# A 3x3 convolution in Winograd form: the first input in two pieces, and the first stores behind copies on VectorE

## The chip, the cores and the metric

The kernel runs on one core of one Trainium2 chip. The metric is the device time of one execution in microseconds (us). The kernel before takes 126.59 us, the median of 3 runs (126.56 to 126.64).

A core has five engines with a queue of their own each: TensorE (PE; its weight loads are shown as PEld), VectorE (DVE), ScalarE (ACT), GpSimd (POOL) and SyncE (SP). Transfers are issued from SP, ACT and POOL and are carried out by 16 DMA engines that all of them share.

## The reference

The input `x` is (16, 64, 64, 64) in f32: 16 images, 64 input channels, 64 rows, 64 columns. The weight is (128, 64, 3, 3). The output is (16, 128, 64, 64) in f32.

```
x_pad = np.pad(x, ((0, 0), (0, 0), (1, 1), (1, 1)), mode='constant')
for b, co, ci, kh, kw:
    output[b, co] += weight[co, ci, kh, kw] * x_pad[b, ci, kh:kh+h, kw:kw+w]
```

## The kernel before

**Tiling.** Two images make a pair: their 2 x 64 channels fill the 128 partitions. There are 8 pairs (p = 0 to 7). A pair is worked in 4 blocks (`blk`) of 8 row pairs, which is 16 output rows. Along the rows a small Winograd form is used: the sum of two neighbouring input rows (tile `ss`, f16) is multiplied by the middle weight row (`G1`) and gives U; the odd and even output rows are U plus products of single input rows (tile `xs`, f16) with differences of weight rows (`G21`, `G0` for group A, `G01`, `G2` for group Bt).

**One block** (lines 120 to 182). TensorE computes U (6 matmuls: 3 columns of the weights by 2 images, from `ss`), then A (12 matmuls, from `xs`), then Bt (12 matmuls, from `xs`), each into two PSUM tiles `acc`, one for each image. ScalarE copies U out of PSUM (`ut`, line 164). VectorE adds `ut` to A (line 174) and to Bt (line 177) and writes the f32 result tiles `ot`, one for each image of the pair (64 rows, 2 MB). A block's U needs the row sums of that block; its A and Bt need the f16 rows of the block and one row beyond each end.

**Stores.** When a pair's fourth block is done, SP stores the first image's `ot` (line 181). The second image's store is put into the list `held` and issued on ACT in the next block, behind that block's copies of U (line 171). The last pair is stored in halves.

**Inputs.** Pairs 0 to 3 come as f32 over the SP queue: the weights (line 42), then all of `x0` in one transfer of 2 MB (line 45), then `xf` of pairs 1, 2 and 3 (line 49). Pairs 4 to 7 come over the POOL queue with a cast to f16 on the way straight into `xs` (`load`, line 67): `load(4)` ahead of the pair loop, `load(5)` to `load(7)` in pairs 1 to 3, each behind the row sums that GpSimd makes for the next pair (lines 112 to 116, helper line 76).

**The start.** TensorE transposes the weights (line 93), ScalarE casts them (line 94), then TensorE runs 10 matmuls on zeros (`spin(10)`, line 95). GpSimd makes the two differences of weight rows (lines 96 and 97) and issues `load(4)`. VectorE makes the row sums of all four blocks of pair 0 and ScalarE casts all four pieces of `x0` to f16 (lines 99 to 101), ahead of the pair loop. For pairs 1 to 3 ScalarE casts `xf` in blocks 2 and 3 of the pair before (line 169).

**Order.** `keep` holds an instruction at its written place among the instructions of its engine. Each engine works its queue in that order. `x0`, `xf` and `ot` share one pool of 8 buffers (`opool`, line 36), so that pair 4's results reuse the buffers of pair 0's.

Of the kernel before, what the change touches and what calls it, by code (L numbers as in the profile page):

```python
# [8 lines left out]
F32 = mybir.dt.float32  # L9
# [3 lines left out]
@with_exitstack  # L13
def kernel(
    ctx: ExitStack,
    tc: tile.TileContext,
    x: bass.AP,
    weight: bass.AP,
    out: bass.AP,
):  # L20
    nc = tc.nc
    B, CI, H, W = x.shape
    CO = weight.shape[0]
    assert H == 64 and W == 64 and CI == 64 and CO == 128 and B % 2 == 0
    NP = B // 2
    RB = 8

    keep = tc.keep_in_program_order
    x_rows = x.rearrange("b c h w -> (b c) h w")
    out_rows = out.rearrange("b co h w -> b co h w")  # L30
    w_flat = weight.rearrange("co ci kh kw -> co (ci kh kw)")

    const = ctx.enter_context(tc.tile_pool(name="const", bufs=1))
    psum = ctx.enter_context(tc.tile_pool(name="psum", bufs=8, space=bass.MemoryType.PSUM))
    xpool = ctx.enter_context(tc.tile_pool(name="xpool", bufs=5))
    opool = ctx.enter_context(tc.tile_pool(name="opool", bufs=8))
    spool = ctx.enter_context(tc.tile_pool(name="spool", bufs=3))
    upool = ctx.enter_context(tc.tile_pool(name="upool", bufs=4))


    w_raw = const.tile([CO, CI * 9], F32)
    nc.sync.dma_start(w_raw, w_flat)
    x0 = opool.tile([128, H, W], F32, tag="ot", name="x0")
    cuts = [(0, 18), (18, 34), (34, 50), (50, 64)]
    nc.sync.dma_start(x0, x_rows[0:128, :, :])
    xf = {}
    for p in (1, 2, 3):
        xf[p] = opool.tile([128, H, W], F32, tag="ot", name="xf")
        nc.sync.dma_start(xf[p], x_rows[128 * p : 128 * p + 128, :, :])
    zeros = const.tile([128, 512], F16)  # L50
    keep(nc.vector.memset(zeros, 0.0))  # L51
    warm = psum.tile([128, 512], F32, tag="acc", name="warm")

    def spin(n):
        for _ in range(n):
            keep(nc.tensor.matmul(warm, zeros[:, 0:128], zeros))  # L56

    ident = const.tile([128, 128], F16)
    make_identity(nc, ident)
    w16 = const.tile([CO, CI * 9], F16)  # L60
    keep(nc.gpsimd.tensor_copy(w16, w_raw))  # L61

    xs = {p: xpool.tile([128, H, W], F16, tag="xs", name="xs") for p in range(4)}

    def load(p):
        xs[p] = xpool.tile([128, H, W], F16, tag="xs", name="xs")
        keep(nc.gpsimd.dma_start(xs[p], x_rows[128 * p : 128 * p + 128, :, :]))  # L67

    ss = {}

    def sums(eng, p, src, lo, n):
        if p not in ss:
            ss[p] = spool.tile([128, H // 2, W], F16, tag="ss", name="ss")
        v = src.rearrange("p (j i) c -> p j i c", i=2)
        keep(
            eng.tensor_add(  # L76
                ss[p][:, lo : lo + n, :], v[:, lo : lo + n, 0, :], v[:, lo : lo + n, 1, :]
            )
        )


    Wt = const.tile([128, 5, 3, CO], F16)
    G0, G21, G1, G01, G2 = range(5)

    def wrow(i):
        return Wt[:, i, :, :].rearrange("p t c -> p (t c)")

    for kh, g in ((1, G1), (2, G2), (0, G0)):
        wp = psum.tile([128, 512], F32, tag="acc", name="wp")
        for k in range(3):  # L90
            t = 3 * kh + k
            for q in (0, 64):
                keep(nc.tensor.matmul(wp[q : q + 64, k * CO : k * CO + CO], w16[:, t::9], ident))  # L93
        keep(nc.scalar.copy(wrow(g), wp[:, 0 : 3 * CO]))  # L94
    spin(10)
    keep(nc.gpsimd.tensor_sub(wrow(G21), wrow(G2), wrow(G1)))  # L96
    keep(nc.gpsimd.tensor_sub(wrow(G01), wrow(G0), wrow(G1)))  # L97
    load(4)
    for n, (lo, hi) in enumerate(cuts):
        sums(nc.vector, 0, x0, RB * n, RB)  # L100
        keep(nc.scalar.copy(xs[0][:, lo:hi, :], x0[:, lo:hi, :]))  # L101

    held = []

    def store(eng, p, b2, ot, lo, hi):
        return eng.dma_start(
            out_rows[2 * p + b2, :, lo:hi, :],
            ot.rearrange("p j i c -> p (j i) c")[:, lo:hi, :],
        )

    for p in range(NP):
        if p + 1 < NP:
            for lo in (0, 16):
                sums(nc.gpsimd, p + 1, xf.get(p + 1, xs[p + 1]), lo, 16)
        if p > 0 and p + 4 < NP:
            load(p + 4)
        ots = [
            opool.tile([128, H // 2, 2, W], F32, tag="ot", name="ot") for _ in range(2)
        ]
        for blk in range(4):  # L120
            j0 = blk * RB

            def group(wi_rows):

                tiles = [
                    psum.tile([128, RB, W], F32, tag="acc", name="acc") for _ in range(2)
                ]
                n = 3 * len(wi_rows)
                i = 0
                for wi, off in wi_rows:  # L130
                    for kw in (1, 0, 2):
                        c_lo, c_hi = max(0, 1 - kw), min(W, W + 1 - kw)
                        for b2 in range(2):
                            p0 = 64 * b2
                            lo, hi = j0, j0 + RB
                            if off is None:
                                rhs = ss[p][p0 : p0 + 64, lo:hi, c_lo + kw - 1 : c_hi + kw - 1]
                            else:
                                while 2 * lo + off < 0:
                                    lo += 1  # L140
                                while 2 * (hi - 1) + off > H - 1:
                                    hi -= 1
                                first = 2 * lo + off
                                last = 2 * (hi - 1) + off
                                rhs = xs[p][
                                    p0 : p0 + 64,
                                    first : last + 1 : 2,
                                    c_lo + kw - 1 : c_hi + kw - 1,
                                ]
                            nc.tensor.matmul(  # L150
                                tiles[b2][:, lo - j0 : hi - j0, c_lo:c_hi],
                                Wt[p0 : p0 + 64, wi, kw, :],
                                rhs,
                                start=i == 0,
                                stop=i == n - 1,
                            )
                        i += 1
                return tiles

            U = group([(G1, None)])  # L160
            us = []
            for b2 in range(2):
                ut = upool.tile([128, RB, W], F32, tag="ut", name="ut")
                keep(nc.scalar.copy(ut, U[b2]))  # L164
                us.append(ut)
            if p + 1 in xf:
                q = p + 1
                for lo in {2: (0, 16), 3: (32, 48)}.get(blk, ()):
                    keep(nc.scalar.copy(xs[q][:, lo : lo + 16, :], xf[q][:, lo : lo + 16, :]))  # L169
            while held:  # L170
                keep(store(nc.scalar, *held.pop(0)))
            A = group([(G21, 1), (G0, -1)])
            for b2 in range(2):
                nc.vector.tensor_add(ots[b2][:, j0 : j0 + RB, 0, :], A[b2], us[b2])  # L174
            Bt = group([(G01, 0), (G2, 2)])
            for b2 in range(2):
                nc.vector.tensor_add(ots[b2][:, j0 : j0 + RB, 1, :], Bt[b2], us[b2])  # L177
            parts = {3: (0, 64)} if p < NP - 1 else {1: (0, 32), 3: (32, 64)}
            if blk in parts:
                lo, hi = parts[blk]  # L180
                store(nc.sync, p, 0, ots[0], lo, hi)
                held.append((p, 1, ots[1], lo, hi))
    while held:
        keep(store(nc.scalar, *held.pop(0)))
# [30 lines left out]
```

## Time and profile before

| | |
|---|---|
| median of the runs | 126.59 us |
| span of the profiled execution | 124.8 us |
| PE busy | 108.2 us (87%) |
| DVE busy | 82.8 us (66%) |
| ACT busy | 52.0 us (42%) |
| POOL busy | 36.2 us (29%) |
| moved by DMA | 46.57 MB, mean 373 GB/s |
| read from HBM, written to it | 17.07 MB, 33.55 MB |
| granted TensorE clock, mean | 0.963 |

The profiled execution spans 124.8 us from its first to its last instruction; the runs' time is 1.8 us longer than that, for what lies around the span. The page of the profile gives the busy time of each engine, the span in 40 slices of 3.12 us with tenths of busy time, the DMA queues with their share of the 16 engines, the chain of work that ended last, and groups of instructions. In the queue lines q1 is what SP issues, q10 what ACT issues and q0 what POOL issues. A casting load counts there with the bytes that it writes (1 MB in f16) and not with the 2 MB that it reads. The view by windows gives the same for chosen stretches; the timeline gives instructions in order of time, with the idle time ahead of them and what ended it.

### The profile page before, as it was taken

The page shows a single profiled execution, that of the slowest core. Times are in us where ns is not written, and L with a number is a line of the kernel's source. Part 1 is how long each engine was busy: PE and PEld are TensorE (multiplying, and loading weights), DVE is VectorE, ACT ScalarE, POOL GpSimd, SP SyncE. Part 2 cuts the span into 40 slices and gives each one's busy share as a digit, 9 for nine tenths or more (in the row PEclk, how much of TensorE's full clock was granted, in tenths as well). Part 3 has the DMA queues.
Part 4 walks back from the last instruction along what each step waited for, and adds up shares of the span by engine and source line. Part 5 has one row for each costly group of instructions (what it writes and reads, how often), then busy time and mean ns, then how long its engine had stood idle before and what let it go on. Part 6 is the DMA issues. An engine that isn't in the chain of part 4 may idle for free.

```text
span 124.8 us, 2437 instructions
## 1 busy us (share of the span) xinstructions
PE 108.2 (87%) x988; PEld 49.3 (40%) x988; DVE 82.8 (66%) x133; ACT 52.0 (42%) x84; POOL 36.2 (29%) x27
## 2 busy tenths in 40 slices
PE   0699999999999999999999999999999999990000
PEld 0433444444444444444444444444444444440000
DVE  0016787878878787877777778777877787685000
ACT  4319749833993399333333333333333333330000
POOL 2360086294799202920067000940000000000000
PEclk9999999999999999999999999999999999999555
DMA  6899999999999999999999999999999999999991
GB/s 173 362 436 407 297 323 349 425 315 415 397 349 368 305 376 373 360 334 362 381 347 360 334 344 412 431 431 425 425 441 420 436 415 425 436 412 418 436 402 74
DMA packets 3898, 46.57 MB, mean 373 GB/s; under 512 B 432, under 2 KB 432, under 8 KB 560
## 3 DMA queue, kind: packets, MB, share of 16 engines
q1 hardware_dynamic: 2016, 25.46, 49.5%
q10 hardware_dynamic: 1296, 16.78, 31.6%
q0 software_dynamic: 576, 4.19, 16.1%
q8 instruction: 7, 0.11, 0.3%
q14 instruction: 3, 0.02, 0.0%
HBM read 17.07 MB, written 33.55 MB: 406 GB/s over the span
## 4 chain that ended last, share of the span: by engine, by line
PE 86%; DMA 2%; DVE 1%; issue 1%; POOL 1%; DVEq 0%
PE acc L150 81%; PE warm L56 4%; DMA w_raw<-in_weight_dram 2%; PE wp L93 1%; DVE ot L174 1%; POOL w L61 1%; DVE ot L177 0%; DVEq L210 0%; DVEq L174 0%
## 5 line engine op out<-in xcount | busy, mean ns | idle before, releaser
L150 PE MATMUL acc<-xs,Wt 64*128 64x504 f16 (+3 forms) x768 | 87.0, 373 | 0.0
L150 PEld LDWEIGHTS <-Wt 64*128 64x128 f16 x960 | 46.8, 94 | 56.2 <-issue 0.8
L164 ACT COPY ut<-acc 128x512 f32<-128x512 f32 x64 | 34.3, 588 | 52.9 <-issue 32.1
L174 DVE TENSOR_TENSOR ot<-acc,ut 128x512 f32<-128x512 f32 x64 | 41.2, 686 | 22.6 <-PE acc L150 18.3
L177 DVE TENSOR_TENSOR ot<-acc,ut 128x512 f32<-128x512 f32 x64 | 41.1, 684 | 0.0
L150 PE MATMUL acc<-ss,Wt 64*128 64x504 f16 (+1 forms) x192 | 26.0, 377 | 0.0
L76 POOL TENSOR_TENSOR ss<-xs 128x1024 f16<-128x1024 f16 x8 | 16.8, 2124 | 20.2 <-DMA xs<-in_x_dram 20.2
L76 POOL TENSOR_TENSOR ss<-xf 128x1024 f16<-128x1024 f32 x6 | 14.1, 2361 | 13.6 <-DMA xf<-in_x_dram 13.6
L169 ACT CAST xs<-xf 128x1024 f16<-128x1024 f32 x12 | 12.0, 1058 | 0.0
L76 DVE TENSOR_TENSOR ss<-x 128x512 f16<-128x512 f32 x4 | 2.5, 687 | 7.7 <-DMA x<-in_x_dram 7.7
L93 PE MATMUL wp<-ident,w 128*64 128x128 f16 x18 | 1.3, 328 | 4.3 <-POOL w L61 4.3
L101 ACT CAST xs<-x 128x1024 f16<-128x1024 f32 (+2 forms) x4 | 3.9, 1042 | 2.6 <-DMA x<-in_x_dram 2.6
L67 POOL DMA_DIRECT2D xs<-in_x_dram x4 | 2.4, 600 | 7.8 <-ACT xs L169 7.8
L56 PE MATMUL warm<-zeros 128*128 128x512 f16 x10 | 4.4, 631 | 0.0
L93 PEld LDWEIGHTS <-w 128*64 128x64 f16 x18 | 1.1, 210 | 4.3 <-POOL w L61 4.3
L94 ACT CAST Wt<-wp 128x384 f16<-128x384 f32 x3 | 1.2, 487 | 2.9 <-PE wp L93 2.9
L56 PEld LDWEIGHTS <-zeros 128*128 128x128 f16 x10 | 1.3, 143 | 2.3 <-issue 2.2
L94 ACT ACT_TABLE_LOAD x1 | 1.3, 1283 | 0.7 <-PEq L199 0.7
L96 POOL TENSOR_TENSOR Wt<-Wt 128x384 f16<-128x384 f16 x1 | 0.9, 907 | 1.7 <-ACT Wt L94 1.7
L61 POOL CAST w<-w_raw 128x576 f16<-128x576 f32 x1 | 0.7, 663 | 2.3 <-DMA w_raw<-in_weight_dram 2.3
L97 POOL TENSOR_TENSOR Wt<-Wt 128x384 f16<-128x384 f16 x1 | 0.9, 910 | 0.0
L51 DVE MEMSET zeros<- 128x256 uint32 x1 | 0.3, 272 | 0.9 <-PEq L199 0.9
(6 smaller groups left out, 0.9 us busy)
## 6 DMA issues: line engine op xcount, KB each, us to landing
out_dram<-ot SPq DMA_DIRECT2D x7, 2048.0 KB, 22.0
out_dram<-ot ACTq DMA_DIRECT2D x7, 2048.0 KB, 18.9
xf<-in_x_dram SPq DMA_DIRECT2D x3, 2048.0 KB, 22.1
xs<-in_x_dram POOLq DMA_DIRECT2D x4, 1024.0 KB, 23.4
x<-in_x_dram SPq DMA_DIRECT2D x1, 2048.0 KB, 7.6
out_dram<-ot SPq DMA_DIRECT2D x2, 1024.0 KB, 10.6
out_dram<-ot ACTq DMA_DIRECT2D x2, 1024.0 KB, 11.0
w_raw<-in_weight_dram SPq DMA_DIRECT2D x1, 288.0 KB, 2.8
```

What stands on the lines that cost most here:

```text
L56: keep(nc.tensor.matmul(warm, zeros[:, 0:128], zeros))
L61: keep(nc.gpsimd.tensor_copy(w16, w_raw))
L67: keep(nc.gpsimd.dma_start(xs[p], x_rows[128 * p : 128 * p + 128, :, :]))
L76: eng.tensor_add(ss[p][:, lo : lo + n, :], v[:, lo : lo + n, 0, :], v[:, lo : lo + n, 1, :])
L93: keep(nc.tensor.matmul(wp[q : q + 64, k * CO : k * CO + CO], w16[:, t::9], ident))
L94: keep(nc.scalar.copy(wrow(g), wp[:, 0 : 3 * CO]))
L101: keep(nc.scalar.copy(xs[0][:, lo:hi, :], x0[:, lo:hi, :]))
L150: nc.tensor.matmul(tiles[b2][:, lo - j0 : hi - j0, c_lo:c_hi], Wt[p0 : p0 + 64, wi, kw, :], rhs, start=i == 0, stop=i == n - 1,)
L164: keep(nc.scalar.copy(ut, U[b2]))
L169: keep(nc.scalar.copy(xs[q][:, lo : lo + 16, :], xf[q][:, lo : lo + 16, :]))
L174: nc.vector.tensor_add(ots[b2][:, j0 : j0 + RB, 0, :], A[b2], us[b2])
L177: nc.vector.tensor_add(ots[b2][:, j0 : j0 + RB, 1, :], Bt[b2], us[b2])
```

## The change

- `x0` comes in two transfers, rows 0 to 17 and rows 18 to 63, on the same SP queue.
- Of the matmuls on zeros 6 stand ahead of the weight transposes and 2 behind them, in place of 10 behind.
- A GpSimd copy of one column out of row 63 of `x0` (`hold`) stands ahead of `load(4)`, which thereby waits for the second piece of `x0`.
- Of the four row sums and four casts of pair 0, only the first of each stands ahead of the pair loop. Each of the others is made one block ahead of its use, inside pair 0: the cast on ACT behind the copies of U, the sum on VectorE between the adds of A and the adds of Bt.
- The adds of A and Bt get `keep`.
- Pair 0's two stores are not issued at its end. In pair 1, block 1, behind the first add of A, VectorE copies one element column of each of pair 0's two result tiles onto itself; then SP stores the first tile and, behind the second add, ACT the second.

```diff
-    nc.sync.dma_start(x0, x_rows[0:128, :, :])
+    for lo, hi in ((0, 18), (18, H)):
+        nc.sync.dma_start(x0[:, lo:hi, :], x_rows[0:128, lo:hi, :])
...
+    spin(6)
     for kh, g in ((1, G1), (2, G2), (0, G0)):
...
-    spin(10)
+    spin(2)
     keep(nc.gpsimd.tensor_sub(wrow(G21), wrow(G2), wrow(G1)))
     keep(nc.gpsimd.tensor_sub(wrow(G01), wrow(G0), wrow(G1)))
+    hold = const.tile([128, 1], F32)
+    keep(nc.gpsimd.tensor_copy(hold, x0[:, H - 1, 0:1]))
     load(4)
-    for n, (lo, hi) in enumerate(cuts):
-        sums(nc.vector, 0, x0, RB * n, RB)
+
+    def first_cast(n):
+        lo, hi = cuts[n]
         keep(nc.scalar.copy(xs[0][:, lo:hi, :], x0[:, lo:hi, :]))
 
+    sums(nc.vector, 0, x0, 0, RB)
+    first_cast(0)
+
     held = []
+    gate = []
...
+            if p == 0 and blk < 3:
+                first_cast(blk + 1)
...
             for b2 in range(2):
-                nc.vector.tensor_add(ots[b2][:, j0 : j0 + RB, 0, :], A[b2], us[b2])
+                keep(nc.vector.tensor_add(ots[b2][:, j0 : j0 + RB, 0, :], A[b2], us[b2]))
+                if gate and blk == 1 and b2 == 0:
+                    for ot in gate:
+                        end = ot[:, H // 2 - 1, 1, W - 1 : W]
+                        keep(nc.vector.tensor_copy(end, end))
+                    store(nc.sync, 0, 0, gate[0], 0, H)
+                    held.append((0, 1, gate[1], 0, H))
+                    gate = []
+            while p == 1 and held:
+                keep(store(nc.scalar, *held.pop(0)))
+            if p == 0 and blk < 3:
+                sums(nc.vector, 0, x0, j0 + RB, RB)
             Bt = group([(G01, 0), (G2, 2)])
             for b2 in range(2):
-                nc.vector.tensor_add(ots[b2][:, j0 : j0 + RB, 1, :], Bt[b2], us[b2])
+                keep(nc.vector.tensor_add(ots[b2][:, j0 : j0 + RB, 1, :], Bt[b2], us[b2]))
...
-            if blk in parts:
+            if blk == 3 and p == 0:
+                gate = ots
+            elif blk in parts:
```

## The prediction

> **What bounds the kernel now.** I read the page first. Its chain of waits gives TensorE 86% of the span, but the slices say otherwise:
>
> ```profile
> PE   0699999999999999999999999999999999990000
> DMA  6899999999999999999999999999999999999991
> q1 hardware_dynamic: 2016, 25.46, 49.5%
> q10 hardware_dynamic: 1296, 16.78, 31.6%
> q0 software_dynamic: 576, 4.19, 16.1%
> PE 86%; DMA 2%; DVE 1%; issue 1%; POOL 1%; DVEq 0%
> ```
>
> TensorE stops four slices before the end; the DMA engines are full from the third slice to the last but one, and the three queues' shares sum to 97.2%. Windows show how full:
>
> ```profile
> 1.00:2.00 1.00, 0.00 (x0) 0.00 (x0) 0.13 (x1) 1.00 (x1) 0.29 (x1) 1.00 0.23 44
> 24.00:26.00 2.00, 2.00 (x22) 0.98 (x20) 1.40 (x3) 0.70 (x2) 1.70 (x1) 1.00 1.13 442
> 26.00:28.00 2.00, 2.00 (x22) 0.88 (x18) 1.39 (x3) 1.07 (x2) 2.00 (x2) 1.00 0.94 246
> 30.00:32.00 2.00, 2.00 (x22) 0.93 (x20) 1.27 (x4) 1.97 (x4) 0.16 (x1) 1.00 1.02 434
> 115.00:120.00 5.00, 0.00 (x0) 0.00 (x0) 0.00 (x0) 0.00 (x0) 0.00 (x0) 0.57 1.01 428
> ```
>
> The last two columns are the DMA share and GB/s. VectorE is done at 113.9 us; from there to 124.8 us only transfers run, at 428 GB/s, so the two last stores (2.1 MB, 4.9 us at that rate) stand behind older ones. **The transfers are the bound:** the change leaves their bytes alone, so the end moves only with time in which the 16 engines stand idle or run slowly. TensorE has slack: the bytes left at 113.9 us take some 9 us, of which 4.9 us are the last stores' own, so it could end about 4 us later.
>
> One stretch is slow: 26 to 28 us moves 246 GB/s at a full share. Against 430 that loses 0.9 us, and 28 to 29 us (328 GB/s) another 0.2: 1.1 us in all. The queue view explains when stores begin:
>
> ```profile
> DMA packets 22, 0.20 MB, mean 393 GB/s; under 512 B 10, under 2 KB 10, under 8 KB 10
> ## 3 DMA queue, kind: packets, MB, share of 16 engines
> q1 hardware_dynamic: 21, 0.18, 85.8%
> q10 hardware_dynamic: 1, 0.02, 7.6%
> ```
>
> This is 28.5 to 29 us: the first ACT store packet, though ACT issued it at 24.30. From 26 to 28 us only q1 moves, with loads. So pair 0's stores, issued early, wait in their queues until the loads are through and follow without a gap. By bytes: the windows sum to 11.27 MB by 32 us; loads are 9.73 MB of it, 0.03 is instructions. The 1.5 MB of stores take 3.5 us at 430 GB/s: **stores effectively start at 28.5 us.** From there to the end both kernels move the same bytes without a pause. So I forecast one time: when the stores' first bytes move after the change.
>
> **The change, part by part.** The rows I use:
>
> ```profile
> 1.17 0.42 SPq L45 DMA_DIRECT2D x<-in_x_dram  x1
> 8.80 2.50 DVE L76 TENSOR_TENSOR ss<-x 128x512 f16<-128x512 f32 x4 [7.67 <-DMA x<-in_x_dram]
> 9.92 0.82 PE L150 MATMUL acc<-ss,Wt 64*128 64x512 f16 x6
> 16.33 0.81 PE L150 MATMUL acc<-ss,Wt 64*128 64x512 f16 x6
> 18.55 1.29 DVE L174 TENSOR_TENSOR ot<-acc,ut 128x512 f32<-128x512 f32 x2 [0.47 <-PE acc L150]
> 23.70 0.35 SPq L106 DMA_DIRECT2D out_dram<-ot  x1
> 28.11 1.29 DVE L174 TENSOR_TENSOR ot<-acc,ut 128x512 f32<-128x512 f32 x2 [0.73 <-PE acc L150]
> 31.84 4.68 POOL L76 TENSOR_TENSOR ss<-xf 128x1024 f16<-128x1024 f32 x2 [2.35 <-DMA xf<-in_x_dram]
> ```
>
> *The first piece of x0.* The weights land at about 3.5 us. 18 rows are 0.59 MB, 1.4 us at 430 GB/s: landed near 4.9. The second piece lands where the whole did, 8.8; the extra issue costs SP 0.42 us, hidden while the DMA is backed up. Sum 0 (0.69 us) ends at 5.6. ACT's three weight casts end at 6.2, its cast of 18 rows (1.15) at 7.35. The transposes end at 5.6, two spins (0.43 each) at 6.4: first U at 6.4, not 9.92. The six spins ahead run from about 1.2 to 3.8, while PE waits for the weights until 4.30. A begins at 7.35, after the cast (G21 is ready at 6.82).
>
> *Pair 0 then runs by VectorE.* Each later U needs its sum, and VectorE makes that behind both adds of A. From a U to the first A add is 2.22 us (16.33 to 18.55), both adds 1.29, the sum 0.69 less 0.05 overlap, the hand-over about 0.1 (an estimate from the 0.05 to 0.1 us between such rows): 4.2 us a block, where Us stand 3.24 apart now (13.09, 16.33, 19.58). A add 0: A begins at 7.35, 12 matmuls and the tail of the last take about 1.5: 8.8; adds to 10.05, sum 1 to 10.7, U of block 1 at 10.8 (13.09 before). Blocks 2 and 3: 15.0 and 19.2. Pair 1: 22.4 and, block 1, 25.6, against 22.74 and about 25.9. The early start is given back almost entirely; TensorE ends 0.3 us earlier, in its slack.
>
> *The gate.* Pair 1's first A add in block 1 ends at 25.6 + 2.22 + 0.68 = 28.5; then two copies of one column. The trace has none on VectorE: below, nothing; above, the 0.27 us of its memset; I take 0.1 each, like GpSimd's 128x1 memsets, which are the nearest in size. They delay the second add inside the 0.73 us that VectorE idles there. SP issues at 28.6. From issue to the first bytes: the weights were issued at 0.74 on empty queues, and the window 1 to 2 us holds a share of 0.23, so data moves from 1.77: 1.0 us. **First store bytes at 29.6, 1.1 us later than the 28.5 of now.** The loads, if the slow stretch goes with the early stores, end at 27.4, and the engines stand empty for 2.2 us; if it stays, at 28.5 and for 1.1. The end is the same.
>
> *Other waits.* Behind the gated store SP has only pair 1's store (36.5). ACT waits until 28.7 with nothing behind but the U copies of block 2, ready after 29.4. POOL's copy waits until 8.8, so `load(4)` goes out 1.3 us later (7.63 before); pair 4 needs it past 60 us, and meanwhile xf fills the engines. That copy's own time, 0.1 to 0.66 us by GpSimd's nearest rows, lies in POOL's wait for xf. `load(5)` stands behind sums that wait for xf, issued near 28.9 as now, too late to fill the hole. Casts: block 2 holds ACT for 1.07 + 0.93 + 2 x 1.0 = 4.0 us, within 4.2. If xf of pair 1 came late here, TensorE's slack pays, but the gate moves with it. Pair 4 reuses pair 0's buffers near 60 us; their stores land about 1 us after 45.7, no wait.
>
> *Clock.* TensorE spins 0.43 us apart up to 9.37 and runs 512 columns in 0.21 from 9.92: full speed 5.1 to 5.6 us after its first work at 4.30. From 1.2 us on that gives 6.3 to 6.8, so U and some of A may run at half: 0 to 0.6 us later at the gate; I take 0 and keep 0.6 for the range. The Trainium skill's page TensorE: Matmul & The Clock Gate, Part 1, states that a free-running window of about 3.4 us has to be busy first: by it, as an estimate, full speed comes one to two windows after the first work, at 4.6 to 8.0 us, and the sum is 1.1 or, at 8.0, 1.7; the 5.1 to 5.6 us of this trace lie between one and two windows.
>
> Span: 124.8 + 1.1 = 125.9. The profiled span lies 1.8 us below the runs' median; with that, **127.7 us**, 0.9% slower.
>
> **Rivals.** *Faster: the slow stretch goes and no hole opens.* If sums and adds on VectorE don't hold pair 0 and Us stand 3.24 apart from 10.0, the gate's add ends at 10.0 + 2 x 3.24 + 3.2 + 3.2 + 2.9 = 25.8; stores queue up by 26.8, ahead of the loads' end at 27.4. Then the 1.1 us come back: 125.5. It decides at the gate: SP's issue before 26.4. For it: the slow stretch begins some 1.5 us after the first two stores' issue and never recurs. Against: 2.22, 1.29 and 0.69 are firm rows in one chain. Chance 0.18.
>
> *Same: late engines set the end.* One transfer is done only when the slowest of 16 engines is; pair 3's xf releases POOL at 31.84, 2.8 us after q1 turned to stores elsewhere. An engine with loads left until past 29.6 has no hole, and if it also ends last, the end stays: 126.6. Against: its loads share it with stores from 28.5, so its real lag is about half. The Trainium skill's DMA: Bandwidth & Descriptors, Latency and other measured facts, says engines 7 and 15 are usually slower; the 31.84 fits one slow engine, but not which. Chance 0.12.
>
> *Much slower: the pieces don't act as pieces.* If sum 0 waits for all of x0, U starts at 9.9 again, A's adds end at 13.5, U of block 1 is at 14.3, all 3.5 us later: 127.7 + 3.5 = 131.2. For it: a wait may cover a whole tile; against: A started at 10.58, before ACT's last cast into the same xs. Chance 0.12.
>
> **Numbers.** Forecast 0.58, its own range 127.1 (late engines absorb half of 1.1) to 128.8 (1.1, and 0.6 for the clock, 0.2 for a dearer copy, 0.3 for hand-overs of 0.2 three times). The range takes in the faster case and leaves out 131.2: 125.5 to 128.8. By over 0.2% (0.25 us, about what a measurement here can tell): faster 0.18, same 0.12, slower 0.70.
>
> **What would show it.** Right: Us of pair 0 near 6.4, 10.8, 15.0, 19.2; DVE, not PE, as releaser before them; SP's first store near 28.6; a window near 28 to 29.5 us with a low DMA share and TensorE busy; from 30 us full shares to the end. Wrong: full shares through 27 to 30 us, store issue before 26.4, or an end that no longer follows the DMA.

## The result, and the profile after

The kernel after takes 131.2 us (median of 4 runs, 130.51 to 131.37) against 126.58 us before: a ratio of 1.0358, interval 1.0341 to 1.0376. It is 4.6 us slower, where 1.1 us were forecast; the time lies above the range. The profiled execution spans 129.6 us against 124.8. Medians and ranges here are of all executions, ratios of the fast ones alone, because some executions of the same kernel, of the kernel before too, are over 1.5% longer.

Lines from the page of the kernel after: slices and chain.

```profile
PE   6897649999999999999999999999999999980000
DVE  0109694687878777877778778777877787772000
PEclk9999995999999999999999999999999999999755
DMA  4999999964999999999999999999999999999990
PE 81%; DVE 5%; DMA 2%; issue 2%; POOL 1%; DVEq 0%
```

Two things are new. The DMA row, full throughout before, drops to 6 and 4 in the ninth and tenth slice (26 to 32 us, at 3.24 us a slice). And TensorE is weak in the fourth to sixth (7, 6, 4; 10 to 19 us), with a slice of low clock behind it; in the chain VectorE has 5% in place of 1. The timeline shows where this comes from:

```profile
11.06 0.68 DVE L77 TENSOR_TENSOR ss<-x 128x512 f16<-128x512 f32 x1
...
15.07 5.10 POOL L77 TENSOR_TENSOR ss<-xf 128x1024 f16<-128x1024 f32 x2 [4.67 <-DMA xf<-in_x_dram]
15.21 2.75 DVE L77 TENSOR_TENSOR ss<-x 128x512 f16<-128x512 f32 x1
...
18.01 0.82 PE L159 MATMUL acc<-ss,Wt 64*128 64x512 f16 x6 [2.80 <-DVE ss L77]
...
23.19 0.82 PE L159 MATMUL acc<-ss,Wt 64*128 64x512 f16 x6
...
32.51 0.35 SPq L115 DMA_DIRECT2D out_dram<-ot  x1
```

The same row sum on VectorE takes 0.68 us at 11.06 and 2.75 us at 15.21, just behind GpSimd's first row sum. TensorE waits 2.80 us for it. The next block then takes 5.2 us (18.01 to 23.19) in place of the 4.2 forecast, and SP issues the first store at 32.51, not 28.6. The windows give the clock and the transfers; the last three columns are granted clock, DMA share and GB/s:

```profile
16.00:18.00 2.00, 0.00 (x0) 0.00 (x0) 2.00 (x2) 0.00 (x0) 2.00 (x2) 1.00 1.01 311
...
20.00:22.00 2.00, 2.00 (x12) 0.75 (x10) 0.76 (x2) 2.00 (x3) 0.17 (x1) 0.50 1.08 332
...
26.00:28.00 2.00, 2.00 (x22) 0.96 (x20) 1.90 (x4) 1.80 (x4) 2.00 (x2) 1.00 0.96 410
28.00:30.00 2.00, 2.00 (x24) 0.92 (x20) 1.51 (x3) 0.32 (x1) 2.00 (x2) 1.00 0.08 33
30.00:32.00 2.00, 2.00 (x22) 0.93 (x20) 1.27 (x3) 1.07 (x2) 1.98 (x2) 1.00 0.64 61
...
34.00:36.00 2.00, 2.00 (x22) 0.88 (x18) 1.36 (x3) 2.00 (x4) 1.55 (x2) 1.00 0.97 176
```

From 16 to 18 us TensorE does nothing; from 20 to 22 us it runs at half clock (12 matmuls in place of 22). From 28 to 31 us the DMA engines are almost empty: the loads are through, the stores not yet issued. Then comes a surprise: the stores are issued at 32.5, but from 32.5 to 36.5 us the queues hold this:

```profile
DMA packets 90, 0.75 MB, mean 186 GB/s; under 512 B 0, under 2 KB 0, under 8 KB 0
## 3 DMA queue, kind: packets, MB, share of 16 engines
q0 software_dynamic: 89, 0.73, 102.9%
q8 instruction: 1, 0.02, 1.5%
```

Only `load(5)` moves (POOL issued it at 29.76). The first store packet starts at 36.9 us, 4.4 us behind its issue. (A casting load counts with the bytes that it writes: 16 engines with packets of 8 KB at 0.62 us make 211 GB/s, so 186 is near what this load can show.) Weighing each packet by the usual duration of its kind (0.61 us for 16 KB, 0.62 us for 8 KB of a casting load), the engines lose some 4.5 us between 28 and 38 us; before, they lost about 1 us in the slow stretch and next to nothing from there to the tail. A further 0.6 us against the kernel before is lost from 2 to 6 us, where the first piece of `x0` moves in smaller packets (1.27 MB in these 4 us against 1.53). Together that is some 4.1 us of the 4.8 us by which the span grew; the rest I can't place.

### The profile page after: what moved, and what is told of

Its sections match the earlier page's. It is cut to its first block, busy times and chain, and to the rows that moved or that the text cites. A ratio compares the mean times of both kernels' runs of the same rounds, so it can differ in the third digit from the quotient of the medians.

```text
span 129.6 us, 2437 instructions
## 1 busy us (share of the span) xinstructions
PE 110.7 (85%) x986; PEld 49.5 (38%) x986; DVE 85.3 (66%) x135; ACT 52.0 (40%) x84; POOL 37.3 (29%) x28
## 3 DMA queue, kind: packets, MB, share of 16 engines
q10 hardware_dynamic: 1296, 16.78, 30.5%
## 4 chain that ended last, share of the span: by engine, by line
PE 81%; DVE 5%; DMA 2%; issue 2%; POOL 1%; DVEq 0%
PE acc L159 79%; DVE ss L77 3%; DMA w_raw<-in_weight_dram 2%; DVE ot L185 2%; PE wp L95 1%; PE warm L57 1%; POOL w L62 1%; DVE ot L199 0%; DVEq L234 0%; DVEq L185 0%
## 5 line engine op out<-in xcount | busy, mean ns | idle before, releaser
L159 PE MATMUL acc<-xs,Wt 64*128 64x504 f16 (+3 forms) x768 | 89.0, 380 | 0.0
L159 PEld LDWEIGHTS <-Wt 64*128 64x128 f16 x960 | 47.5, 96 | 62.3 <-issue 4.3
L173 ACT COPY ut<-acc 128x512 f32<-128x512 f32 x64 | 34.4, 589 | 58.7 <-issue 37.7
L159 PE MATMUL acc<-ss,Wt 64*128 64x504 f16 (+1 forms) x192 | 26.7, 385 | 3.6 <-DVE ss L77 3.6
L77 DVE TENSOR_TENSOR ss<-x 128x512 f16<-128x512 f32 x4 | 4.8, 1201 | 4.8 <-DMA x<-in_x_dram 4.8
L57 PE MATMUL warm<-zeros 128*128 128x512 f16 x8 | 3.8, 628 | 1.2 <-DVE zeros L52 1.2
```

The costliest lines, as they stand in the source:

```text
L77: eng.tensor_add(ss[p][:, lo : lo + n, :], v[:, lo : lo + n, 0, :], v[:, lo : lo + n, 1, :])
L159: nc.tensor.matmul(tiles[b2][:, lo - j0 : hi - j0, c_lo:c_hi], Wt[p0 : p0 + 64, wi, kw, :], rhs, start=i == 0, stop=i == n - 1,)
```

## The experiments

For reference, the start of the first stores in all the kernels, in us. "Bytes" is the start of the first store packet in the trace's DMA records; in the kernels that issue ahead of 28 us (before, e1, e4, e6, e8, e9) it is that of ACT's first large store, since SP's stores can't be told from its loads there. Issue, bytes and span are of the one profiled execution, the time is the median of all. The profiled execution took less than its median in e2 (128.43), e5 (130.43) and e13 (130.11), and more in e3 (129.1) and e9 (128.17).

| kernel | SP issue | load(5) issue | bytes | span | time |
|---|---|---|---|---|---|
| before | 23.70 | 28.93 | 28.6 | 124.8 | 126.58 |
| e4, a small store early | 23.44 | 29.09 | 28.3 | 124.6 | 126.64 |
| e6, extra instructions | 23.35 | 29.29 | 28.1 | 124.9 | 126.63 |
| e1, all but the gate | 24.53 | 29.71 | 28.7 | 124.6 | 126.73 |
| e9, x0 in pieces alone | 24.56 | 30.25 | 28.7 | 126.4 | 126.67 |
| e8, gate a block earlier | 26.06 | 28.93 | 28.1 | 125.9 | 127.56 |
| e2, gate alone | 28.61 | 29.14 | 29.5 | 126.7 | 129.04 |
| e3, sums early | 28.95 | 29.38 | 29.8 | 127.3 | 127.77 |
| e10, turns taken | 29.12 | 29.59 | 30.0 | 127.4 | 129.22 |
| e5, spins in the wait | 29.62 | 29.69 | 30.5 | 128.4 | 131.68 |
| e11, later start | 30.10 | 29.57 | 34.3 | 129.0 | 130.75 |
| e12, the same and spins | 30.20 | 29.71 | 34.4 | 129.1 | 131.01 |
| e13, e11 with load(5) later | 30.10 | 34.68 | about 31 | 128.3 | 131.06 |
| after | 32.51 | 29.76 | 36.9 | 129.6 | 131.2 |
| e7, after with load(5) later | 32.74 | 34.70 | 33.6 | 131.0 | 129.66 to 134.0 |

### e1: all of the change but the gate

```diff
-            while p == 1 and held:
-                keep(store(nc.scalar, *held.pop(0)))
...
-            if blk == 3 and p == 0:
-                gate = ots
-            elif blk in parts:
+            if blk in parts:
```

> The kernel after, without the wait of pair 0's stores: they are issued at the end of pair 0 again (SP near 27.3 us, since pair 1 starts at 26.4 there). Theory L: the first stores of the program move their first bytes some 4.6 us after issue whatever stands in the queues (4.6 us in the kernel after), so near 31.9 us, and the DMA engines stand empty from 28.4 to there: 127.8 us (127.2 to 128.8). Rival Q: the 4.6 us came of the casting load that stood in the queues, and stores alone start 1.0 us after issue: near 28.4 us, no hole, 126.9 us.

126.73 us, ratio 1.0024 (0.9981 to 1.0066): the same as before. SP issued at 24.53 us and not at 27.3, because pair 0 ended earlier here: the sum of block 2 began at 14.22 us, ahead of GpSimd's (15.12), and took 0.68; the sum of block 3 fell under GpSimd's second and took 1.94:

```profile
15.12 4.67 POOL L77 TENSOR_TENSOR ss<-xf 128x1024 f16<-128x1024 f32 x2 [4.68 <-DMA xf<-in_x_dram]
...
18.39 1.94 DVE L77 TENSOR_TENSOR ss<-x 128x512 f16<-128x512 f32 x1
```

(The 4.6 us of the expectation are 4.4 by the packet records.) There was no hole, as rival Q has it, but the stores stood behind loads, so that this run doesn't decide between L and Q. It shows that the new order of pair 0, one slow sum included, costs nothing measurable by itself; it acts through the gate.

### e2: the gate alone

The kernel before, with the diff's lines of `gate` and nothing else.

> The kernel before with the wait of pair 0's stores alone. TensorE's course stays (pair 1, block 1 near 25.9 us), SP issues near 28.9 us. Theory L: first bytes near 33.5 us, the loads end near 27.4, the casting load that POOL issues at 28.9 fills part of the hole: 130.3 us (129 to 131). Rival Q, stores start 1.0 us after issue: near 29.9 us, 128.0 us.

129.04 us, ratio 1.0207 (1.0143 to 1.0271). First store bytes come at 29.5, 0.9 us behind SP's issue: theory L falls, Q stands, and the forecast of 1.0 us from issue to first bytes was right. But 1.0 us of later stores cost 1.8 to 3.4 us of time. The windows, of the fastest of the four executions (128.43 us), show where:

```profile
28.00:30.00 2.00, 2.00 (x22) 1.08 (x20) 2.00 (x6) 0.24 (x1) 1.98 (x3) 1.00 0.38 147
30.00:32.00 2.00, 2.00 (x22) 1.06 (x20) 1.36 (x3) 2.00 (x4) 2.00 (x1) 1.00 0.97 401
...
34.00:36.00 2.00, 2.00 (x22) 1.09 (x20) 1.68 (x3) 1.96 (x3) 1.98 (x3) 1.00 0.79 205
```

The slow stretch has left 26 to 28 us, but another stands at 34 to 36 (205 GB/s), just ahead of the first packets of `load(5)` at 35.5. From 26 to 36 us the engines lose some 2.4 us against 1.0 before, and a few tenths more up to 50, which is about what this execution is longer. That `load(5)` causes the slow stretch is not shown.

### e3: the row sums out of GpSimd's way

```diff
-            if p == 0 and blk < 3:
-                sums(nc.vector, 0, x0, j0 + RB, RB)
+            if p == 0 and blk == 0:
+                for n in (1, 2, 3):
+                    sums(nc.vector, 0, x0, n * RB, RB)
```

> The kernel after with the three later row sums of pair 0 made one behind the other in block 0, ahead of GpSimd's first row sum. Theory: the sum of 2.75 us was slow because GpSimd read SBUF at the same time. Then all four take 0.69 us, Us of pair 0 stand near 6.7, 11.8, 15.1 and 18.3 us, TensorE's clock stays full, SP issues near 27.7 us. With theory L first bytes near 32.3 us and 128.3 us; with rival Q first bytes near 28.7 us and 127.0 us. If the slow sum has another cause, one of the three is slow again.

127.77 us, ratio 1.0114 (1.005 to 1.0178): 3.4 us below the kernel after. The three sums together take 1.89 us; the Us stand at 7.4, 13.2, 16.4 and 19.6. In the execution that was traced, the longest of the four (129.1 us), the first sum is the slow one (1.40 us at 5.93, beside GpSimd's weight differences), and the first U and A run at half clock (7.5 to 10.9 us); SP issues 1.3 us later than expected. The first sum meets the weight differences in every trace of the kernel after and its variants: where it begins first (after, e1, e5, e7) it takes 0.69 us and the difference beside it 1.27 to 1.40 in place of 0.91, and where the difference begins first (e3, e10, e11, e12, e13) the sum takes 1.21 to 1.41.

### e10: the same sums, taken in turns

```diff
+    turn = const.tile([128, 1], F16)
...
-        if p + 1 < NP:
+        if 0 < p < NP - 1:
...
+            if p == 0 and blk == 2:
+                keep(nc.gpsimd.tensor_copy(turn, ss[0][:, H // 2 - 1, 0:1]))
+                for lo in (0, 16):
+                    sums(nc.gpsimd, 1, xf[1], lo, 16)
```

> The kernel after, with GpSimd's first row sums put behind VectorE's last row sum of pair 0 (a copy of one column of that sum on GpSimd makes them wait); nothing else is moved. If the two engines' turns at SBUF are what made the gate late, all of VectorE's sums take 0.7 us, pair 1 starts near 22.5 to 23.5 us, SP's first store is issued near 28.6 to 29.6 us on empty engines, its first bytes move 0.9 us later, and the time is 127.7 to 129 us, with a full clock from 12 us on. GpSimd's sums for pair 1 then end near 22.3 us for the first half, just in time. If TensorE's idle time has another cause: 131.2 us.

129.22 us, ratio 1.0153 (1.0076 to 1.0229), 2.0 us below the kernel after. No instruction of VectorE was moved, and its sums of blocks 2 and 3 are quick:

```profile
14.89 0.68 DVE L77 TENSOR_TENSOR ss<-x 128x512 f16<-128x512 f32 x1
...
19.06 0.68 DVE L77 TENSOR_TENSOR ss<-x 128x512 f16<-128x512 f32 x1
...
19.95 4.69 POOL L77 TENSOR_TENSOR ss<-xf 128x1024 f16<-128x1024 f32 x2
```

The sum of block 2 proves little, since at 14.89 us it began ahead of the time (15.0 to 15.2) at which GpSimd's first sum begins in the other kernels. The sum of block 3 does: in e11 below, where GpSimd's two sums were left in place (15.22 to 20.17), the same sum begins at nearly the same time and is slow:

```profile
19.12 1.60 DVE L77 TENSOR_TENSOR ss<-x 128x512 f16<-128x512 f32 x1
```

So it is GpSimd's sum beside it that makes VectorE's slow.

### e6: the two engines' turns by themselves

```diff
+            if p in (1, 6) and blk in (0, 3):
+                extra = const.tile([128, RB, W], F16, name=f"extra{p}{blk}")
+                if blk == 0:
+                    keep(nc.vector.tensor_add(extra, us[0], us[1]))
+                else:
+                    keep(nc.vector.tensor_scalar_mul(extra, us[0], 2.0))
```

> The kernel before with four extra instructions on VectorE, 512 elements each, whose results are not used: in pair 1 and in pair 6, an add of two SBUF tiles in block 0 and a product of one SBUF tile with 2 in block 3. GpSimd makes row sums beside those of pair 1 and nothing beside those of pair 6. Theory (two SBUF inputs on VectorE and a GpSimd instruction that reads SBUF take turns): the add takes 0.7 us in pair 6 and 1.0 to 2.9 us in pair 1, or GpSimd's sum is longer by as much; the one-input product is a smaller question: the same time in both pairs if one input never waits. Rival (the slow sum came from x0 or from its place in the queue): the add takes 0.7 us in both.

```profile
24.22 5.12 POOL L76 TENSOR_TENSOR ss<-xf 128x1024 f16<-128x1024 f32 x2 [4.08 <-DMA xf<-in_x_dram]
...
25.74 1.38 DVE L178 TENSOR_TENSOR extra<-ut 128x512 f16<-128x512 f32 x1
...
35.45 1.60 DVE L180 TENSOR_SCALAR extra<-ut 128x512 f16<-128x512 f32 x1
...
89.76 0.68 DVE L178 TENSOR_TENSOR extra<-ut 128x512 f16<-128x512 f32 x1
...
99.48 0.42 DVE L180 TENSOR_SCALAR extra<-ut 128x512 f16<-128x512 f32 x1
```

The add takes 1.38 us beside GpSimd's sums and 0.68 without; GpSimd's two sums take 5.12 us in place of 4.69. The one-input product waits too: 1.60 against 0.42. The adds that read PSUM (1.29 for two) keep their time beside GpSimd throughout. The rival, that `x0` or the place mattered, falls. The times say how the two share: in the kernel after, e1, e11 and here, VectorE's sum or add ends 0.55 us after the end of the GpSimd sum that had begun before it (here 27.12 us after 26.57), whenever it began itself.

### e5, e11, e12: the clock

e5 puts 8 matmuls on zeros into TensorE's wait (the first hunk); e11 starts later by 4 zeros matmuls in place of 2 (the second); e12 has both.

```diff
+            if p == 0 and blk == 2:
+                again = psum.tile([128, 512], F32, tag="acc", name="again")
+                for _ in range(8):
+                    keep(nc.tensor.matmul(again, zeros[:, 0:128], zeros))
...
-    spin(2)
+    spin(4)
```

> The kernel after with 8 matmuls on zeros ahead of U of block 2 in pair 0, where TensorE stood idle for 2.8 us and then ran at half clock from 18.9 to 22.5 us. If the clock fell because of that idle time, it stays full here: U of block 3 comes near 22.3 us instead of 23.2, SP's first store near 31.6 instead of 32.5, and the time falls by 0.5 to 0.9 us against the kernel after, to 130.3 to 130.7 us. If the clock does not matter to the end: 131.2 us. The slow sum stays in either case.

> The kernel after with 4 matmuls on zeros in place of 2 behind the weight transposes: the first U comes some 0.4 to 0.9 us later, so that the sum for block 2 always starts behind GpSimd's row sum of 15.1 us. If that sum's start against GpSimd's decides, it takes 2 us or more as in the kernel after, TensorE waits about 2.8 us and its clock falls to half again: 131.2 to 132 us, SP's first store near 32.5 to 33 us.

> The same with 8 matmuls on zeros ahead of U of block 2 in pair 0, inside the wait for the slow sum. The slow sum stays; if the clock fell because of the idle time, it stays full now, pair 0 ends 0.9 to 1.9 us earlier than in the kernel with the later start alone, and the time lies 0.5 to 1.5 us below that kernel's. If the clock has no part in the end: the same time.

131.68 us for e5 (ratio 1.0392, 1.0323 to 1.0462), 130.75 for e11 (1.0322, 1.0275 to 1.0369), 131.01 for e12 (1.0346, 1.0303 to 1.0389). The expectations failed in their premise: in the profiled executions of e5 and e12 no sum of blocks 2 and 3 was slow, and in e11 only that of block 3 was (1.60 us at 19.12). With 4 zeros matmuls the first U came 0.7 us later (7.45 us, held up by a first sum of 1.25 us), but it ran at full clock, so that the first A add came at 9.58 and not behind 9.85. So these runs don't isolate the clock's share. They show something else: in e11 the clock stays full, SP issues at 30.10, 2.4 us earlier than in the kernel after, and the time is almost the same. What e11, e12 and the kernel after share is that `load(5)` was issued ahead of the stores.

### e7 and e13: load(5) out of the stores' way

```diff
-        if p > 0 and p + 4 < NP:
-            load(p + 4)
+        if p == 2:
+            load(5)
+        if p > 1 and p + 4 < NP:
+            load(p + 4)
```

> The kernel after with load(5) issued together with load(6), so that no casting load stands in the queues when pair 0's stores are issued near 32.5 us. Theory Q (a transfer starts 1.0 us after issue on empty engines, and some 4 us after issue behind another queue's work): first store bytes near 33.5 us instead of 36.9. The engines then stand empty from 28.5 to 33.5 us, 5 us against the 4.5 us lost in the kernel after: 131 to 132 us. If the 4.4 us belong to the stores themselves: first bytes near 37 us, and 134 to 135 us.

> The kernel with 4 matmuls on zeros in place of 2 (SP issued its first store at 30.1 us there, 0.5 us behind load(5), and stores moved from 34.3 us on: 130.75 us), with load(5) issued together with load(6) as well. If the order of load(5) and the first stores costs time of its own, stores move from 31.0 us on, the engines lose 3.0 to 3.5 us between 28 and 36 us in place of 4.3, and the time is 129.5 to 130 us. If only the time of the gate matters, since load(5) has to be moved at some time anyway: 130.75 us or more.

In e7, traced in a run of 132.81 us, SP issues at 32.74 and the first bytes move at 33.6, 0.9 us later, and so do they in e13 (30.10 to 31.0): the 4.4 us belong to the queues, not to the stores. The runs of e7 spread from 129.66 to 134.0 us, so its time decides nothing. In e13, with the gate at e11's time, the engines lose some 2.5 us between 28 and 36 us in place of 4.3, as the first theory had it; but between 36 and 50 us they lose over 1 us more than in e11, when `load(5)` starts behind the stores. The time, 131.06 us (ratio 1.0363, 1.0323 to 1.0404), can't be told from e11's. So no cost of the order by itself shows: in both, the engines stand empty from 28 us until something is issued, and lose time again when the other starts.

### e4, e8 and e9: the slow stretch

e4 is the kernel before with one small store into the output issued on ACT at the start; e8 is e2 with `blk == 0` for `blk == 1`; e9 is the kernel before with `x0` in two pieces and nothing else.

> The kernel before with one store of 64 bytes a partition into the output, issued on ACT at the start (those 16 columns are written again by the last store). Theory L in the form that the first store into the output is slow and slows what runs beside it: the slow stretch at 26 to 28 us goes, pair 0's stores follow the loads at 27.5 us, 125.5 us. If the delay belongs to each large store or to the queues' first large store: the slow stretch stays, 126.6 us.

> The kernel before with the copies and pair 0's stores one block earlier than in the change, in block 0 of pair 1: SP issues near 25.5 us, while the loads still run until 27.4. In the run without the gate stores issued at 24.5 us had no slow stretch. If the slow stretch depends on issue while more than about 4 us of loads stand queued, it goes, no hole opens, and the time is 125.7 us. If the stores start some 4 us after issue as they do behind loads, near 29.5 us, a hole of up to 2 us opens and takes the place of the slow stretch: 126.5 to 127.5 us.

> The kernel before with x0 loaded in the two pieces of 18 and 46 rows and nothing else. In the kernel after the engines moved 355 GB/s from 4 to 6 us against 401 before. If the pieces themselves cost that, some 0.5 us are lost there: 127.1 us; the slow stretch at 26 to 28 us stays. If the loss came of something else at the start: 126.6 us.

e4: 126.64 us, ratio 1.0008 (0.9983 to 1.0034), and the slow stretch stays (287 GB/s from 26 to 28 us): it does not hang on the first store into the output. e8: 127.56 us with a wide spread (126.25 to 128.5; ratio 1.0034, 0.9995 to 1.0073), so not faster. No hole opens at 28 us and the slow stretch is gone there, but 0.4 us are lost from 32 to 36 and 0.5 from 36 to 50. e9: 126.67 us, ratio 0.9994 (0.9964 to 1.0023). In its trace the pieces cost some 0.6 us from 2 to 6 us, and the slow stretch at 26 to 28 us is gone (401 GB/s). That the one pays for the other would fit the equal times, but is not shown: the execution traced here was 1.5 us longer than the median. e1, which has the pieces too and was traced in a run of 126.43 us, shows both:

```profile
2.00:4.00 2.00, 1.93 (x5) 0.45 (x3) 0.00 (x0) 0.01 (x1) 0.33 (x1) 1.00 0.99 298
4.00:6.00 2.00, 1.61 (x19) 1.26 (x20) 0.20 (x1) 0.96 (x3) 0.35 (x2) 1.00 1.03 345
...
26.00:28.00 2.00, 2.00 (x22) 0.88 (x18) 2.00 (x4) 0.37 (x1) 2.00 (x2) 1.00 0.97 401
```

The kernel before moves 363, 401 and 246 GB/s in these three windows. The pieces don't do away with slow stretches as such: e3 and e10 have one at 34 to 36 us (262 and 266 GB/s), as e2 has. What the slow stretch is stays open; no kernel tried was faster than the one before.

## Why the prediction was wrong

**What held.** The direction, and the way to it: a late gate and a hole in the transfers. The transfers are the bound: TensorE's last work and VectorE's (117.5 us) again lie 12 us ahead of the end. The early start is given back: in e10, with quick sums, the Us are 4.2 us apart as forecast (11.47, 15.63, 19.80), and pair 1 starts at 22.97 where 22.4 was forecast and 22.74 stood before. The hole, and its place from 28 us on, came as forecast. A store issued on empty engines moves its first bytes 0.9 us later (e2, e3, e7, e10), against 1.0.

**The step that failed: "the sum 0.69 less 0.05 overlap".** The duration was read from the row at 8.80 us, beside which GpSimd makes nothing, and moved to a place beside GpSimd's row sums of pair 1, which I had in view only as a consumer of xf. There it took 2.75 us. The Trainium skill's page SBUF — State Buffer, section SBUF: two separate sides, says that a VectorE instruction with two SBUF inputs and a GpSimd instruction that reads SBUF take an exclusive lock on a shared pair of ports, and that the one that comes second is blocked for the whole instruction of the other. This trace agrees: GpSimd's first sum runs from 15.07 to 17.40 us; VectorE's, begun at 15.21, ends at 17.96, 0.55 us later. I didn't look for it. With the sums out of each other's way the time is 2.0 us (e10) to 3.4 us (e3) lower, of the 3.5 us by which the forecast was too low. The step fails at the forecast's own times too: there the sum of block 3 begins near 18.4 us, where e1's took 1.94.

**The clock, taken at 0 with 0.6 in reserve.** TensorE's matmuls came 0.43 us apart until 8.8 us, through U and the first third of A, and 0.21 apart from there on; the first A add came at 9.85, not 8.8. In e1 they were 0.21 us apart from U's start at 6.55 us on, and the add came at 8.87. That one us moved the sum of block 2 from ahead of GpSimd's sum (14.2 in e1) to behind it (15.21): a small term decided which sum was caught. The second fall of the clock, from 19.0 to 22.4 us, followed the 2.8 us wait and wasn't in the prediction; it makes the block 5.2 us long where e10's blocks take 4.2. No run isolates its effect on the time.

**The gate.** Together these put SP's issue at 32.51 in place of 28.6. The Us of pair 0 show the parts: block 1 stands at 11.79 where 10.8 was forecast (1.0 us, the start), block 2 at 18.01 for 15.0 (2.0 us more, the slow sum), block 3 at 23.19 for 19.2 (1.0 us more, the half clock); the 4 us then stay up to the gate.

**"From there to the end both kernels move the same bytes without a pause."** In e2 the first bytes moved 1.0 us later than before, and the time rose by 2.6 (1.8 to 3.4); a slow stretch stood again at 34 to 36 us, when `load(5)` started behind the stores. So even with the gate at the forecast's time the 1.1 us forecast were too few, by some 1.5 us. In the kernel after it worked the other way: from 28.5 to 36.9 us is 8.4 us, but only some 4.5 us were lost, since `load(5)`, which I had called too late for the hole, moved in it.

**The rivals.** *Much slower* gave 131.2 us, the time that was measured, by coincidence: its mechanism did not occur, for the first sum began at 5.94 us, right behind the first piece. *Faster* failed where it was said to be decided, at the gate (26.4). *Same* had no part: the hole shows in the mean of all engines.

## What to carry to other kernels

A duration moves with its neighbours: before an instruction is put somewhere else, look at what the engine that shares its ports does at that time, not only at whether its own inputs are ready. Where transfers are the bound, a wait ahead of a store is safe only while something else still stands in the queues; a gate on a compute chain moves with that chain, here by 4 us, and later stores cost more than their delay (e2). A wait on the transfer's own progress was not tried. A forecast that ends 1 us short of another engine's start should carry what happens behind it as a case of its own.

## What the runs showed that I had not expected

Beside GpSimd's row sums a VectorE instruction with one f32 input in SBUF waited as well (1.60 us against 0.42, in e6), while adds with one input in PSUM did not.

A transfer issued while another queue keeps the engines busy starts late: 4.4 us behind its issue for the stores of the kernel after, 4.2 in e11, and some 6.4 us for `load(5)` behind the stores in e2 (29.14 to 35.5), against 0.9 us for stores and 1.3 us for `load(5)` (29.57 to 30.9 in e11) on empty engines. The Trainium skill's DMA: Bandwidth & Descriptors, Queues, rings and completion order, has each engine change in turn between the queues that have work; the shares once all are under way fit that (39.0, 30.6 and 27.4% for three queues from 37 to 39 us in the kernel after), but in the newcomer's first microseconds none of its packets move. Whether the engines had its work by then, no trace shows.

The clock fell to half after 2.8 us without a matmul (kernel after) and stayed full after 2.0 us (e1); whether the length or the moment of the wait decided, no run isolates.
